# Fourier part of a small transformer: half-width token transform, then sum and difference of cosine and sine parts

## The chip, the cores and the metric

The kernel runs on one core of one Trainium2 chip. The metric is the device time of one execution in microseconds. The kernel before takes 1688.06 us, the median of three runs (1687.9 to 1688.19).

## The reference, cut to what matters

The program is four transformer blocks on one input sequence of 256 tokens and width 1024, in fp32. The first two blocks (layers 0 and 1) carry a context sequence of 256 tokens beside it; their mixer has three branches, whose outputs are joined and projected:

```python
fx = fourier_mix(col(ux, OFF_FOURIER, FOURIER_W), w_four[l])
ax, ac = attention_group(ux, uc, ...)
rx, rc = hgrn_group(ux, uc, ...)
x = x + g_a * (jnp.concatenate([fx, ax, rx], axis=-1) @ w_out[l])
```

The change touches the first branch only. It is a two-dimensional Fourier transform of a real input, over the 256 tokens and over the 64 features of each of four groups, of which the real part is kept, and then a product with a weight of 256 x 256:

```python
z = u.astype(jnp.float32).reshape(b, n, FOURIER_GROUPS, FOURIER_GD)
z = jnp.fft.fftn(z, axes=(1, 3), norm="ortho").real
return z.reshape(b, n, FOURIER_W).astype(u.dtype) @ w
```

In layer 0 it is computed for the context and for the input sequence, in layer 1 for the input sequence alone: three calls in all. The two later blocks have no Fourier part.

## The kernel before, in words

Matmul operands of the large products are split into a high and a low part (`split`, L170 on ScalarE and L171 on VectorE) and multiplied in three matmuls (`mm3`, L177 to L179). The Fourier part uses plain fp32 matmuls instead. Each fp32 matmul appears in the trace as two passes, each with a weight load of its own.

`mix1` builds layers 0 and 1. Its steps come in the order of the string `STEPS`: the recurrent branch (`z`, `h`), then `k`, `q`, `u`, `g` (projections; `u` fills the Fourier input `uf`), `m` (the output tile `mT`), `a` (attention) and `r` (`hgrn_read`, the read-out of the recurrent branch, whose transposes are L1312). The Fourier calls stand after all steps. Behind `mix1` comes the out projection, whose first two k tiles are the Fourier rows of `mT`; in layer 0 one more modulation job (`ada_late`, matmuls L321) stands between them in the program.

The order on each engine is not the program's. The tile framework takes, for each engine, the ready instruction that is first in the program, by its own estimate of durations; later work can so run ahead of earlier work that waits. The eight PSUM banks have fixed duties: `mm` 0 to 3 (products and attention scores), `tr` 4 and 5 (transposes), `ac` 6 (the attention's value products), `qk` 7. A bank is taken by `tr_bank()` or `qk_bank()` and is free again when its last reader is done.

The attention (`attention`, `softmax`, `pv`) works in sets of 512 score columns: scores L1512 into an `mm` bank, minimum L934 on VectorE, exponential L944 on ScalarE, reciprocal L955, scaling L959 (ScalarE) or L961 (VectorE), four transposes L897 into a `tr` bank, a copy to SBUF (L902 VectorE, L904 ScalarE). After four heads the passes of the value product L970 follow (8 for the context, 16 for the input sequence), and its split into `mT`. Layer 0 has 8 sets for the context and 16 for the input sequence, layer 1 has 16.

One Fourier call (`fourier`, L1063) has three products. The token transform (L1071) multiplies the 256 tokens of `uf` with the table `dft` of 256 cosine and 256 sine columns, in two halves of 128 features, each into bank 7 and from there by a copy into `a` (`foua`). The feature transform multiplies `a` with the block-diagonal tables `bd`: cosines (L1077) and, accumulating in the same bank, negated sines (L1078); a copy makes `z` (`fouz`). The weight product (L1084) follows in bank 7 again, and `split` writes the result to `mT`. `copy` (L164 or L166) alternates between ScalarE and VectorE from call to call.

Of the kernel before, what the change touches and what calls it, by code (L numbers as in the profile page):

```python
# [12 lines left out]
F32 = mybir.dt.float32  # L13
# [7 lines left out]
P = 128  # L21
# [26 lines left out]
def shape_constants():  # L48

    n = np.arange(SEQ)  # L50
    freqs = 10000.0 ** (-np.arange(0, 32, 2, dtype=np.float64) / 32)
    cos = np.zeros((SEQ, 64))
    sin = np.zeros((SEQ, 64))
    for off, pos in ((0, n // 64), (32, n % 64)):
        ang = pos[:, None] * freqs
        cos[:, off : off + 16] = cos[:, off + 16 : off + 32] = np.cos(ang)
        sin[:, off : off + 16] = -np.sin(ang)
        sin[:, off + 16 : off + 32] = np.sin(ang)
    ang = 2 * np.pi * ((n[:, None] * n[None]) % SEQ) / SEQ
    dft = np.concatenate([np.cos(ang), np.sin(ang)], 1)  # L60
    m = np.arange(64)
    ang = 2 * np.pi * ((m[:, None] * m[None]) % 64) / 64
    norm = 1.0 / math.sqrt(SEQ * 64)
    bd = np.zeros((P, 2, P))
    for g in range(2):
        s = slice(g * 64, g * 64 + 64)
        bd[s, 0, s] = np.cos(ang) * norm
        bd[s, 1, s] = -np.sin(ang) * norm
    t = np.arange(P) % 64
    mask = np.zeros((P, 7, 64), np.uint32)  # L70
    s_, t_ = t[:, None], m[None]
    for i, b in enumerate(LEVELS):
        mask[:, i] = (s_ // (2 * b) == t_ // (2 * b)) & (s_ // b != t_ // b)
    mask[:, 6] = s_ == t_
    dist = np.abs(n[:, None] - n[None])
    d_a = np.where(dist <= 128, dist, FAR)
    pos = np.arange(SEQ)
    tok = 2 * (pos % 128) + pos // 128
    dist = np.abs(tok[:, None] - tok[None])
    d_b1 = np.where(dist <= 64, dist, FAR)  # L80
    d4 = np.where(tok[:P, None] % 4 == tok[None, :P] % 4, dist[:P, :P], FAR)
    d16 = np.where(tok[:P, None] % 16 == tok[None, :P] % 16, dist[:P, :P], FAR)
    d_b23 = np.concatenate([d4, d16], 1)
    f = lambda a: np.ascontiguousarray(a, np.float32)
    return {
        "k_rope": f(np.stack([cos, sin], 1)),
        "k_dft": f(dft),
        "k_bd": f(bd),
        "k_mask": np.ascontiguousarray(mask),
        "k_dist": f(np.concatenate([d_a, d_b1], 1)),  # L90
        "k_dist2": f(d_b23),
    }


class Net:
# [967 lines left out]
    def fourier(self, pool, uf, tiles, mT, col0):  # L1063

        nc = self.nc
        mm = nc.tensor.matmul
        a = self.t(pool, [P, 2, 512], F32, "foua", bufs=1)
        for ft in range(2):
            ps = self.qk_bank()
            for i, tt in enumerate(tiles):  # L1070
                mm(ps, uf[:, tt, ft * P : ft * P + P], self.dft[:, i], start=i == 0, stop=i == 1)  # L1071
            self.copy(a[:, ft], ps)
        z = self.t(pool, [P, 2, 256], F32, "fouz", bufs=1)
        ps = self.qk_bank()
        for ft in range(2):
            o = ps[:, ft * 256 : ft * 256 + 256]
            mm(o, self.bd[:, 0], a[:, ft, :256], start=True, stop=False)  # L1077
            mm(o, self.bd[:, 1], a[:, ft, 256:], start=False, stop=True)  # L1078
        self.copy(z, ps.rearrange("p (f t) -> p f t", f=2))
        ps = self.qk_bank()  # L1080
        for ct in range(2):
            o = ps[:, ct * 256 : ct * 256 + 256]
            for k in range(2):
                mm(o, self.wf[:, k, ct * P : ct * P + P], z[:, k], start=k == 0, stop=k == 1)  # L1084
        cs = slice(col0, col0 + 256)
        self.split(mT[0][:, 0:2, cs], mT[1][:, 0:2, cs], ps.rearrange("p (f t) -> p f t", f=2))
# [268 lines left out]
    def mix1(self, hp, pool, l, hT, start=None, late=None):  # L1355
        nc, A = self.nc, self.A
# [23 lines left out]
        ps = []  # L1380
# [68 lines left out]
        v = self.t(pool, [P, 4, 128], F32, "v", bufs=1)  # L1449
# [78 lines left out]
        uf = gs_["uf"]  # L1528
        hes.close()
        with self.tc.tile_pool(name=f"four{l}", bufs=2) as ap:  # L1530
            self.dft = self.load(ap, "dft", [P, 2, 512], A["k_dft"].rearrange(
                "(t p) n -> p t n", p=P))
            self.bd = self.load(ap, "bd", [P, 2, P], A["k_bd"])
            self.wf = self.load(ap, "wf", [P, 2, 256], A["w_four"][l].rearrange(
                "(k p) n -> p k n", p=P))
            for seq in seqs:
                self.fourier(ap, uf, (2 * seq - t0, 2 * seq - t0 + 1), mT, seq * 256)
            if late is not None:
                for job in late(ap, (4,), 6):
                    for _ in job:  # L1540
                        pass
# [373 lines left out]
```

## Time and profile before

| | |
|---|---|
| time, median of three runs | 1688.06 us |
| the profiled execution | 1694.94 us |
| its span | 1693.1 us |
| PE busy | 1624.1 us (96%) |
| PE weight loads busy | 1342.8 us (79%) |
| VectorE busy | 1222.1 us (72%) |
| ScalarE busy | 855.8 us (51%) |
| mean DMA rate | 183 GB/s |

The page and the rows come from one profiled execution, which took a little longer than the timed runs. PE is the matmul engine, PEld its weight loads, DVE is VectorE, ACT is ScalarE, SPq the queue that issues DMAs. Matmuls are pipelined and their ends are modelled, so records of PE overlap, and its busy time is not the time at its peak.

### The profile page before, as it was taken

What the parts mean: (1) busy time and instruction counts of PE and PEld (TensorE: products, weight loads), DVE (VectorE), ACT (ScalarE), POOL (GpSimd) and SP (SyncE); (2) the same over time, 40 slices, a digit from 0 to 9 for tenths busy, and PEclk for the clock granted to TensorE, in tenths of its full rate; (3) what the DMA queues carried; (4) which work ended last, traced back from release to release, by engine and by line L of the source; (5) the groups of instructions that cost most, each with busy time, mean ns of one, the idle gap of its engine ahead of it and who ended that gap; (6) DMA issues with size and microseconds to landing.
All of it is one profiled execution on the core that took longest, in us unless ns stands there. A gap on an engine that the chain in (4) does not pass through costs nothing.

```text
span 1693.1 us, 27315 instructions
## 1 busy us (share of the span) xinstructions
PE 1624.1 (96%) x10343; PEld 1342.8 (79%) x10343; DVE 1222.1 (72%) x2042; ACT 855.8 (51%) x1697; POOL 45.0 (3%) x53
## 2 busy tenths in 40 slices
PE   7999899999999999899999999999999999889998
PEld 5777667877778877787678899777989988769896
DVE  4558866887978977878768887887776566575555
ACT  4446664533343334555755455686544456564443
POOL 0001100000000000101000000000000000000000
PEclk9999999999999999999999999999999999999999
DMA  9551425664678786522268897533876543255653
GB/s 325 185 175 32 154 76 175 188 193 144 225 233 302 265 267 201 161 85 79 82 198 291 311 312 238 163 124 123 277 249 184 184 133 93 77 175 168 204 176 112
DMA packets 169482, 310.48 MB, mean 183 GB/s; under 512 B 12163, under 2 KB 72819, under 8 KB 169350
## 3 DMA queue, kind: packets, MB, share of 16 engines
q1 hardware_dynamic: 168966, 308.17, 56.4%
q8 instruction: 81, 1.33, 0.3%
q10 hardware_dynamic: 384, 0.56, 0.1%
q14 instruction: 51, 0.42, 0.1%
HBM read 307.64 MB, written 1.05 MB: 182 GB/s over the span
## 4 chain that ended last, share of the span: by engine, by line
PE 69%; DMA 10%; DVE 10%; ACT 6%; issue 3%; POOL 1%; SPq 1%; ACTq 0%; POOLq 0%; DVEq 0%
PE bank L179 18%; PE bank L178 18%; PE bank L177 18%; DVE wlo L171 3%; ACT whi L170 3%; PE bank L970 2%; DMA raw<-w_up 2%; PE bank L897 2%; DMA raw<-ffn_w_in 2%; DMA raw<-w_gate 2%; DMA raw<-w_down 1%; ACT colj L387 1%; PE bank L1512 1%; PE bank L321 1%; DMA raw<-w_in 1%
## 5 line engine op out<-in xcount | busy, mean ns | idle before, releaser
L170 ACT CAST whi<-raw 128x1024 fp32r<-128x1024 f32 (+2 forms) x420 | 401.1, 959 | 524.0 <-PE bank L179 198.7
L171 DVE TENSOR_TENSOR wlo<-raw,whi 128x1024 fp32r<-128x1024 f32 (+2 forms) x420 | 464.4, 1110 | 257.0 <-ACT whi L170 247.3
L177 PE MATMUL bank<-hh,whi 128*128 128x256 f32 (+1 forms) x1240 | 386.3, 312 | 0.0
L178 PE MATMUL bank<-hl,whi 128*128 128x256 f32 (+1 forms) x1240 | 385.9, 311 | 0.0
L179 PE MATMUL bank<-hh,wlo 128*128 128x256 f32 (+1 forms) x1240 | 385.2, 311 | 0.2 <-DVE wlo L171 0.2
L177 PE MATMUL bank<-whi,hh 128*128 128x512 f32 (+2 forms) x720 | 265.6, 373 | 10.4 <-ACT hh L170 5.8
L178 PE MATMUL bank<-wlo,hh 128*128 128x512 f32 (+2 forms) x720 | 264.3, 368 | 2.1 <-DVE wlo L171 2.1
L179 PE MATMUL bank<-whi,hl 128*128 128x512 f32 (+2 forms) x720 | 262.5, 368 | 0.2 <-DVE hl L171 0.2
L178 PEld LDWEIGHTS bank<-hl,whi 128*128 128x128 f32 x1240 | 234.6, 189 | 14.8
L177 PEld LDWEIGHTS bank<-hh,whi 128*128 128x128 f32 x1240 | 234.5, 189 | 14.8
L179 PEld LDWEIGHTS bank<-hh,wlo 128*128 128x128 f32 x1240 | 234.1, 189 | 15.2 <-DVE wlo L171 0.4
L358 DVE SCALAR_TENSOR_TENSOR acc<-adaw,cs,acc 128x1024 f32<-128x1024 f32 x154 | 196.0, 1280 | 14.5 <-DMA adaw<-ada_w 6.8
L178 PE MATMUL bank<-wlo,acth 128*128 128x512 f32 x440 | 173.5, 394 | 0.5 <-DVE wlo L171 0.5
L177 PE MATMUL bank<-whi,acth 128*128 128x512 f32 x440 | 173.4, 395 | 0.0
L179 PE MATMUL bank<-whi,actl 128*128 128x512 f32 x440 | 173.3, 394 | 0.0
L177 PEld LDWEIGHTS bank<-whi,hh 128*128 128x128 f32 x720 | 136.7, 191 | 38.1 <-ACT hh L170 8.5
L179 PEld LDWEIGHTS bank<-whi,hl 128*128 128x128 f32 x720 | 137.4, 191 | 23.8 <-DVE hl L171 3.6
L178 PEld LDWEIGHTS bank<-wlo,hh 128*128 128x128 f32 x720 | 137.7, 191 | 21.8 <-DVE wlo L171 3.4
L178 PEld LDWEIGHTS bank<-wlo,acth 128*128 128x128 f32 x440 | 82.7, 188 | 19.2 <-DVE wlo L171 0.9
L179 PEld LDWEIGHTS bank<-whi,actl 128*128 128x128 f32 x440 | 82.9, 188 | 18.5
L177 PEld LDWEIGHTS bank<-whi,acth 128*128 128x128 f32 x440 | 82.8, 188 | 18.2
L756 DVE TENSOR_TENSOR rtmp<-bank,gate 128x512 f32<-128x512 f32 x68 | 46.5, 686 | 30.0 <-PE bank L179 30.0
(297 smaller groups left out, 1837.1 us busy)
## 6 DMA issues: line engine op xcount, KB each, us to landing
adaw<-ada_w SPq DMA_DIRECT2D x96, 512.0 KB
adaw<-w_ada SPq DMA_DIRECT2D x80, 512.0 KB
raw<-ffn_w_in SPq DMA_DIRECT2D x64, 512.0 KB
raw<-w_down SPq DMA_DIRECT2D x46, 512.0 KB
raw<-ffn_w_out SPq DMA_DIRECT2D x40, 512.0 KB
raw<-w_gate SPq DMA_DIRECT2D x32, 512.0 KB
raw<-w_up SPq DMA_DIRECT2D x32, 512.0 KB
raw<-w_in SPq DMA_DIRECT2D x56, 256.0 KB
```

The source lines that it names most:

```text
L170: a = self.nc.scalar.copy(hi, src)
L171: b = self.nc.vector.tensor_sub(lo, src, hi.bitcast(F32))
L177: mm(out, lh, rh, start=start, stop=False)
L178: mm(out, lh, rl, start=False, stop=False)
L179: mm(out, ll, rh, start=False, stop=stop)
L321: nc.tensor.matmul(ps[h][32 * g : 32 * g + 32], self.cs32[:, k0 + g], raws[g][:, h * 512 : h * 512 + 512], start=k0 == 0, stop=k0 > 0,)
L358: nc.vector.scalar_tensor_tensor(acc, raw, s, acc, op0=ALU.mult, op1=ALU.add)
L387: nc.scalar.activation(junk, ps[:, i * P : i * P + P], AF.Copy, accum_out=cols[:, k : k + 1])
L756: nc.vector.tensor_mul(tmp[:, :nw], ps[:, :nw], gate[:, n0 : n0 + nw])
L897: self.nc.tensor.transpose(ps[:, i * P : i * P + P], ps_in[:, i * P : i * P + P], self.ident)
L970: self.nc.tensor.matmul(o[e * 64 : e * 64 + 64], v, pt[:, e::2, i], start=i == 0, stop=i == len(vs) - 1)
L1512: nc.tensor.matmul(dst, q, ksT[:, i, kv, :nk], start=i == 0, stop=i == 1)
```

## The change

The table `dft` keeps 129 cosine columns (0 to 128) and 127 sine columns (1 to 127). The token transform therefore writes 256 columns for each half of the features, and both halves go to one bank and out of it in one copy. The feature transform writes the product of the cosine columns and that of the sine columns side by side, without accumulating, into a bank of the kind `tr` in place of `qk`. The sine part is copied to SBUF (`odd`) by ScalarE. VectorE copies columns 0 and 128, adds the two parts for columns 1 to 127 and subtracts them, read in reverse order, for columns 129 to 255. The weight product and the split are as before.

```diff
-    dft = np.concatenate([np.cos(ang), np.sin(ang)], 1)
+
+    dft = np.concatenate([np.cos(ang)[:, :129], np.sin(ang)[:, 1:128]], 1)
...
-        a = self.t(pool, [P, 2, 512], F32, "foua", bufs=1)
-        for ft in range(2):
-            ps = self.qk_bank()
-            for i, tt in enumerate(tiles):
-                mm(ps, uf[:, tt, ft * P : ft * P + P], self.dft[:, i], start=i == 0, stop=i == 1)
-            self.copy(a[:, ft], ps)
-        z = self.t(pool, [P, 2, 256], F32, "fouz", bufs=1)
+        a = self.t(pool, [P, 2, 256], F32, "foua", bufs=1)
         ps = self.qk_bank()
         for ft in range(2):
             o = ps[:, ft * 256 : ft * 256 + 256]
-            mm(o, self.bd[:, 0], a[:, ft, :256], start=True, stop=False)
-            mm(o, self.bd[:, 1], a[:, ft, 256:], start=False, stop=True)
-        self.copy(z, ps.rearrange("p (f t) -> p f t", f=2))
+            for i, tt in enumerate(tiles):
+                mm(o, uf[:, tt, ft * P : ft * P + P], self.dft[:, i], start=i == 0, stop=i == 1)
+        self.copy(a, ps.rearrange("p (f t) -> p f t", f=2))
+
+        z = self.t(pool, [P, 2, 256], F32, "fouz", bufs=1)
+        ps = self.tr_bank()
+        v = ps.rearrange("p (f t) -> p f t", f=2)
+        for ft in range(2):
+            mm(v[:, ft, :129], self.bd[:, 0], a[:, ft, :129], start=True, stop=True)
+            mm(v[:, ft, 129:], self.bd[:, 1], a[:, ft, 129:], start=True, stop=True)
+        odd = self.t(pool, [P, 2, 127], F32, "fouo", bufs=1)
+        nc.scalar.copy(odd, v[:, :, 129:])
+        nc.vector.tensor_copy(z[:, :, 0:129:128], v[:, :, 0:129:128])
+        nc.vector.tensor_add(z[:, :, 1:128], v[:, :, 1:128], odd)
+        nc.vector.tensor_sub(
+            z[:, :, 129:256], v[:, :, 1:128][:, :, ::-1], odd[:, :, ::-1]
+        )
         ps = self.qk_bank()
...
-            self.dft = self.load(ap, "dft", [P, 2, 512], A["k_dft"].rearrange(
+            self.dft = self.load(ap, "dft", [P, 2, 256], A["k_dft"].rearrange(
                 "(t p) n -> p t n", p=P))
```

## Rows read from the trace of the kernel before

**Rows 1.** The page, busy time of each engine, its share of the span and instructions.
```profile
PE 1624.1 (96%) x10343; PEld 1342.8 (79%) x10343; DVE 1222.1 (72%) x2042; ACT 855.8 (51%) x1697; POOL 45.0 (3%) x53
```

**Rows 2.** The page, the chain that ended last, share of the span by engine.
```profile
PE 69%; DMA 10%; DVE 10%; ACT 6%; issue 3%; POOL 1%; SPq 1%; ACTq 0%; POOLq 0%; DVEq 0%
```

**Rows 3.** Instructions on the Fourier tiles: duration ns min/median/max, first and last start us.
```profile
L1071 PE MATMUL bank<-dft,uf x24: 590/592/697, 195.7 to 830.0; 128*128 128x512 f32 x24
L242 SPq DMA_DIRECT2D dft<-k_dft x2: 367/394/422, 175.8 to 802.0; - x2
...
L1084 PE MATMUL bank<-fouz,wf x24: 378/379/382, 213.0 to 846.1; 128*128 128x256 f32 x24
...
L164 ACT COPY foua<-bank x3: 575/586/588, 198.4 to 823.2; 128x512 f32<-128x512 f32 x3
L166 DVE COPY foua<-bank x3: 674/682/692, 203.2 to 830.9; 128x512 f32<-128x512 f32 x3
...
L164 ACT COPY uf<-bank x3: 361/363/367, 191.0 to 812.9; 128x256 f32<-128x256 f32 x3
```

**Rows 4.** Windows: PE, PEld, DVE, ACT, POOL busy, PEclk, DMA share, GB/s.
```profile
195.60:245.30 49.70, 49.48 (x285) 31.43 (x285) 39.60 (x96) 39.77 (x105) 3.27 (x2) 1.00 0.06 21
...
816.10:848.30 32.20, 32.13 (x181) 20.23 (x181) 24.38 (x54) 22.59 (x51) 0.00 (x0) 1.00 0.10 33
```

**Rows 5.** The chain of waits in order of time: start us, us, what.
```profile
225.31 0.86 PE bank L1071 x2
...
245.78 0.44 PE bank L1312 x4
...
246.45 1.73 PE bank L1084 x8
248.17 4.17 PE bank L321 x24
...
846.45 1.89 PE bank L970 x14
```

**Rows 6.** Timeline, the read-out in layer 0: start us, us, engine, instruction.
```profile
202.27 0.67 DVE L1308 TENSOR_TENSOR hxh<-hxh,gs 128x512 f32<-128x512 f32 x1
...
242.43 0.60 PE L1312 MATMUL bank<-ident,hxh 128*128 128x128 f32 x4
```

**Rows 7.** Timeline, bank 7 between the two Fourier calls of layer 0.
```profile
194.00 0.41 DVE L166 COPY uf<-bank 128x256 f32<-128x256 f32 x1
...
222.15 0.68 DVE L171 TENSOR_TENSOR hl<-bank,hh 128x512 fp32r<-128x512 f32 x1
...
225.15 1.02 PE L1071 MATMUL bank<-dft,uf 128*128 128x512 f32 x2
```

**Rows 8.** Groups by form, 195 to 248 us, VectorE reading a bank.
```profile
L171 DVE TENSOR_TENSOR hl<-bank,hh 128x256 fp32r<-128x256 f32 x8 | 3.3, 418 | 0.7 <-ACT hh L170 0.6
```

**Rows 9.** Timeline, layer 0, Fourier passes beside attention copies.
```profile
235.89 0.58 ACT L904 COPY pt<-bank 128x512 f32<-128x512 f32 x1
...
236.17 1.02 PE L1071 MATMUL bank<-dft,uf 128*128 128x512 f32 x2
...
239.10 0.69 DVE L902 COPY pt<-bank 128x512 f32<-128x512 f32 x1 [1.71 <-PE bank L970]
...
239.49 0.60 PE L1077 MATMUL bank<-foua,bd 128*128 128x256 f32 x2
```

**Rows 10.** Timeline, layer 1, start of the out projection (idle before and its releaser).
```profile
849.73 0.74 PE L177 MATMUL bank<-whi,hh 128*128 128x512 f32 x2 [1.41 <-ACT whi L170]
...
850.99 0.50 PE L178 MATMUL bank<-wlo,hh 128*128 128x512 f32 x1 [0.53 <-DVE wlo L171]
```

**Rows 11.** Windows in and behind layer 1's out projection, columns as in rows 4.
```profile
852.00:854.00 2.00, 2.00 (x6) 1.57 (x5) 1.21 (x2) 0.00 (x0) 0.00 (x0) 0.50 0.89 261
854.00:856.00 2.00, 2.00 (x7) 1.53 (x7) 0.25 (x1) 1.04 (x1) 0.00 (x0) 0.64 0.93 280
...
870.00:880.00 10.00, 8.16 (x41) 6.19 (x40) 7.37 (x15) 6.98 (x17) 1.11 (x2) 1.00 0.36 105
```

## The prediction

> **What bounds the kernel now.** I read the page first: PE is busy for 96% of the span [rows 1] and holds 69% of the chain that ended last [rows 2]. So a shorter matmul can shorten the kernel, but only where no other wait stands right behind it. Next I asked for the instructions on the Fourier tiles: the token transform (L1071), the feature transform (L1077, L1078) and the weight product (L1084) run from 195.7 us in layer 0 (context and input sequence) and up to 846.1 us in layer 1 (input only) [rows 3]. Both places lie inside the attention. There PE reads 49.48 of 49.70 us busy in layer 0 and 32.13 of 32.20 us in layer 1, ScalarE and VectorE 70 to 80% [rows 4]. The chain of waits in these stretches runs through PE in small pieces, Fourier matmuls among them [rows 5].
>
> The timeline then says why they can stand there. The read-out of the recurrent part (L1307, L1308, then transposes L1312) is ahead of the Fourier part in the program. The input of its transposes is written at 202.27 us, and they run at 242.43 [rows 6]; layer 1 has the same picture. PE's order does not hold them, for L1071, later in the program, runs all the while. They need a "tr" bank (4 or 5), and those go round in program order among the attention's transposes, 24 sets in layer 0 and 16 in layer 1. The Fourier part uses bank 7 ("qk") alone, which the attention does not touch here, so it fills the pauses. Bank 7 itself is handed on in program order: the context's result leaves it at 222.15 + 0.68 = 222.83 us, and the first token transform of the input sequence follows at 225.15, though its operand uf was written at 194.00 [rows 7].
>
> **The change, part by part.** *Matmuls.* An fp32 matmul shows as two passes: 24 records for the 12 calls of L1071 [rows 3]. In the chain a pass of 512 columns takes 0.86/2 = 0.43 us, one of 256 columns 1.73/8 = 0.216 us, one of 128 columns 0.44/4 = 0.11 us [rows 5]. For one sequence the token transform falls from 8 x 0.43 = 3.44 to 8 x 0.216 = 1.73 us, the feature transform from 1.73 to 8 x 0.11 = 0.88 us. No row has 129 or 127 columns or an odd start; a pass lies between 0.11 and 0.216 us, and I take 0.11, the row of nearly the same width. Saved: 1.71 + 0.85 = 2.56 us a sequence, 7.7 us of PE work in all.
>
> *Copies and loads.* The copies of a fall from two of 512 elements (0.59 us on ScalarE, 0.68 on VectorE) to one, and that of z goes [rows 3]. In come a ScalarE copy of 254 elements, nearest row 0.363 us for 256 out of a bank [rows 3]; a VectorE copy of four columns, at most the 0.418 us of 256 [rows 8] and beside the ScalarE copy; and an add and a subtract of 254, nearest the same 0.418. The reversed read has no row; I bound it by 0.418 and twice that, and take 0.418. The load of dft falls from 512 to 256 KB; it is issued at 802.0 us in layer 1 [rows 3], some 17 us ahead of its use, so this gains nothing.
>
> *The new place of the feature transform.* It now takes a "tr" bank, and by [rows 6] gets one only after all attention transposes and the read-out. The weight product waits for it and holds bank 7 from the copy of a on; by [rows 7] the input sequence's chain in layer 0 then waits for the context's. So the feature transforms and weight products move from inside the attention to behind it, and in layer 0 the input sequence's token transform as well. Next comes the out projection, whose first k tiles are the Fourier rows; nothing of it can start sooner.
>
> *What the attention gets back.* Layer 0: its attention holds 16 passes of 0.43, 16 of 0.216 and 8 of 0.216 us (the context's weight product), 12.1 us; 1.7 stay, 10.4 go. The return lies between 0 (only pauses were filled) and 10.4. I followed two of them. A pair of L1071 at 236.17 (to 237.19) holds back the value product, whose last operand was copied at 235.89 + 0.58 = 236.47: 0.65 us. The pair ahead of it costs an estimated 0.24 more, so about 0.9 of 1.72 comes back, 52%. The pair of L1077 at 239.49 costs at most 0.1, for the next transposes wait for the copy that ends at 239.10 + 0.69 = 239.79 anyway [rows 9]. I take 52% for the 7.0 us ahead of 231 us, 0.9 + 0.1 for the rest, and 0.4 for the copies: 5.0 us. Layer 1: 5.2 us go; the last group of heads returns nothing (it waits on its own copies), the one before 0.4, the token transform half of 1.71, the copies 0.2: 1.5 us.
>
> By the matmul rows alone PE is full and all 10.4 + 5.2 us would come back. The Trainium skill (Perfetto Trace Analysis, "Identifying the Most-Contended Engine") warns that matmul busy time is a poor measure, since matmuls are pipelined, and asks for the share of weight loads: 31.43 of 49.70 us, 63% [rows 4]. The trace agrees: a pass that takes 0.216 us of the chain is recorded as 0.379 [rows 3, 5]. By the first reading the sum would be -6.9 us, by the second it is the one below.
>
> *What is added behind it.* Layer 1: after the last value product (846.45 + 1.89 = 848.34 [rows 5]) come the feature transform 0.88 + 0.16 for the end of its last pass, the ScalarE copy 0.41, add and subtract 0.82, weight product 1.73 + 0.2, the split's first half 0.65: 4.85 us to the out projection's first matmul. Today that starts at 849.73, stops after two matmuls for wlo and goes on at 850.99 [rows 10], as if it had started at 850.5, 2.2 us behind. The weight splits that hold it today then lie under the chain. Added: 2.6 us. Layer 0: PE gets 0.88 twice, 1.73 and 1.73 = 5.2 us behind the attention. Of the context's chain (4.85 and the read-out's 0.44 = 5.3 us) PE fills 0.44 + 0.88 + 1.73 and eight passes of L321 at 4.17/24 each [rows 5], 1.4 us; 0.9 us is empty. The second chain lies under the context's out projection. Added: 6.1 us.
>
> *Sum.* Layer 0: -5.0 + 6.1 = +1.1; layer 1: -1.5 + 2.6 = +1.1; together +2.2 us. The profiled execution took 1694.94 us (span 1693.1 and 1.84 around it), so 1697.1 for its like; it lies 6.9 us above the median of the timed runs, 1688.06, and the difference carries over: 1690.3 us.
>
> **The rivals.** *Faster: the attention gives most of it back.* For it: the full PE rows [rows 4], and that each pass gone frees those behind it. Against it: the pair at 239.49. At 80%: layer 0 -8.3 + 6.1, layer 1 -4.2 + 2.6, together -3.8 us: 1684.3; at 100%, -6.9: 1681.2. On the same side lies that "tr" banks are not handed out in program order, and the chain stays inside the attention: 45 to 100% of 7.7 us, 1680.4 to 1684.6. Against that stands the 40 us wait of L1312 [rows 6].
>
> *Clearly slower: a serial tail and the clock.* One mechanism: PE stands idle behind the attention while ScalarE and VectorE make z. If the attention returns only 20% (2.1 and 1.0 us) the tails leave +4.0 and +1.6. On top, the granted clock: behind today's pause for whi and wlo it is 0.50 (1.2 GHz) from 852 to 854 us and 0.64 to 856 [rows 10, 11]; that is 3.4 us at half speed, 1.7 lost. A second such stretch in layer 0 makes +7.3 in all, 1695.4. It decides from a return of about a third down. Against it: at 870 to 880 us PE is idle for 1.84 us and the clock stays at 1.00 [rows 11]. The skill (TensorE: Matmul & The Clock Gate, "HAM oscillation — how this bites in real kernels") has it that bursts with waits between them fall back to the low clock time after time; by that rule the new pauses are paid twice.
>
> **How the numbers follow.** My own case 0.50 (its own range 1686 to 1693.5), the faster rival 0.22, the slower one 0.28. About 0.2% (3.4 us) is what a measurement of this kernel can tell from no change. My case lies 2.2 us above the old median, so 0.07 of it goes to slower and 0.02 to faster, and 0.03 of the faster rival stays within: faster 0.21, within 0.2% 0.44, slower 0.35. The range, 1683.5 to 1695.5, takes in the main figures of both rivals and leaves out the ends, about 0.2.
>
> **What would show it.** Right: L1312 still near the end of the attention and the new L1077/L1078 behind it; in layer 1 the first L177 of the out projection about 5 us behind the last value product; layer 0's attention 4 to 6 us shorter. Wrong: a feature transform in the middle of the attention (bank order); an attention shorter by 8 us or more (PE really full); a pass of 129 columns well over 0.11 us; a second stretch at the low clock.

## The result, and the profile after

The changed kernel takes 1701.39 us (median of 4 runs, 1699.42 to 1705.57) against 1687.98 beside it: ratio 1.0073, 95% interval 1.0052 to 1.0094. Timed once more with other runs of the kernel before (`e8_after_again`) it is 1.0070, 1.0057 to 1.0083, or 11.8 us more (9.6 to 14.0). I had forecast 2.2 us more and a range that ended at 1695.5: the prediction was wrong, in the size and in the class it held likeliest.

The page of the changed kernel, engines and then the chain by engine, answers to [rows 1] and [rows 2] and hardly differs: PE is busy 4.5 us less.

```profile
PE 1619.6 (95%) x10343; PEld 1339.6 (79%) x10343; DVE 1222.7 (72%) x2048; ACT 854.7 (50%) x1697; POOL 45.4 (3%) x53
...
PE 69%; DVE 10%; DMA 9%; ACT 7%; issue 4%; POOL 1%; SPq 0%; ACTq 0%; POOLq 0%; DVEq 0%
```

Lines up to the Fourier part have moved down by one; the token transform is L1073 now, the feature transform L1080 and L1081, the weight product L1093. Instructions on the Fourier tiles of the changed kernel, columns as in [rows 3]:

```profile
L1073 PE MATMUL bank<-dft,uf x24: 377/379/483, 198.1 to 836.2; 128*128 128x256 f32 x24
...
L1080 PE MATMUL bank<-foua,bd x12: 275/276/378, 247.5 to 858.4; 128*128 128x129 f32 x12
...
L1081 PE MATMUL bank<-foua,bd x12: 272/273/274, 247.8 to 858.6; 128*128 128x127 f32 x12
...
L1093 PE MATMUL bank<-fouz,wf x24: 379/379/796, 250.9 to 864.3; 128*128 128x256 f32 x24
L1084 DVE COPY fouz<-bank x3: 154/157/168, 249.9 to 860.3; 128x4 f32<-128x4 f32 x3
L1085 DVE TENSOR_TENSOR fouz<-bank,fouo x3: 412/413/413, 250.0 to 860.4; 128x254 f32<-128x254 f32 x3
L1086 DVE TENSOR_TENSOR fouz<-bank,fouo x3: 412/414/414, 250.3 to 860.7; 128x254 f32<-128x254 f32 x3
```

Apart from layer 1's weight product, of which more below, no instruction is clearly dearer than I took it: the subtract that reads in reverse takes 414 ns, the add 413. And the first starts show the move: no feature transform before 247.5 us, no weight product before 250.9.

Windows of the changed kernel, columns as in [rows 4]: the two attentions, each from its first exponential to the end of its last value product, then the stretch behind layer 0's.

```profile
198.43:247.56 49.13, 41.88 (x253) 25.85 (x251) 37.42 (x91) 37.66 (x101) 4.12 (x2) 1.00 0.05 18
822.00:857.76 35.76, 31.01 (x185) 19.62 (x183) 25.08 (x58) 24.96 (x56) 1.64 (x1) 1.00 0.17 56
...
247.56:266.00 18.44, 17.77 (x94) 12.06 (x94) 5.96 (x12) 3.85 (x8) 0.00 (x0) 1.00 0.43 149
```

The same stretches in the trace of before (to the same two instructions):

```profile
196.09:245.34 49.25, 49.10 (x285) 31.17 (x283) 39.15 (x95) 39.29 (x104) 3.27 (x2) 1.00 0.06 18
812.22:848.32 36.10, 34.71 (x200) 22.31 (x199) 26.51 (x60) 25.97 (x58) 1.64 (x1) 1.00 0.16 56
```

This is the result in four lines: 7.2 us of PE's busy time left layer 0's attention (49.10 to 41.88), and the attention got 0.12 us shorter; in layer 1 3.7 us left it for 0.34. Where the time went is in the groups by line of PE in layer 0's attention of the changed kernel (the last column is PE's idle time before them and what ended it). Nearly all of it is new: before, PE was idle for 0.15 us in this stretch.

```profile
L898 PE MATMUL bank<-ident,prob 128*128 128x128 f32 x96 | 15.2, 282 | 1.9 <-ACT prob L960 1.6 <-DVE pt L903 0.3
L971 PE MATMUL bank<-pt,v 128*64 128x256 f32 x96 | 14.7, 390 | 2.3 <-ACT pt L905 1.2 <-DVE pt L903 1.1
L1521 PE MATMUL bank<-ksT,qsT 128*128 128x512 f32 x32 | 12.3, 454 | 3.1 <-ACT prob L945 3.1
```

What was taken out came back as waits for exponentials (3.1 us), copies (2.6) and divisions (1.6). ScalarE and VectorE are not alone in setting the pace: in the chain of waits over this attention, PE's own attention matmuls hold 58% (L971, L898, L1521), ScalarE 31%, VectorE 4%. First line: the changed kernel, 198.43 to 247.56 us; second: before, 196.09 to 245.34.

```profile
by line: PE bank L971 28.9%; ACT prob L945 21.0%; PE bank L898 18.0%; PE bank L1521 11.3%; issue 5.5%; ACT pt L905 4.9%; ACT prob L960 4.8%; DVE pt L903 2.5%; DVE stat L935 1.4%; ACT foua L165 1.0%; DVE stat L956 0.5%; ACTq L945 0.1%; ACTq 
...
by line: PE bank L970 28.3%; PE bank L897 23.8%; PE bank L1512 20.3%; PE bank L1071 14.5%; PE bank L1084 2.6%; PE bank L1077 2.6%; ACT prob L944 2.6%; PE bank L1078 1.8%; issue 1.6%; ACT pt L904 1.0%; PE bank L177 0.9%; PE bank L1312 0.9%; 
```

Before, the Fourier passes (L1071, L1077, L1078, L1084) held 21% of this chain, some 10 us, and still nothing was won by taking most of them out: where PE finds work to fill a wait, the chain runs through that work.

The chain of waits of the changed kernel, where [rows 5] stand: start us, us, what. The exponential, the copies of the probabilities and PE take turns up to the end of the attention; then the read-out, the transforms and both weight products follow in a row, the second token transform among them.

```profile
242.06 0.79 ACT prob L945 x2
...
243.03 0.65 DVE pt L903
...
244.99 0.59 ACT pt L905
...
245.62 1.94 PE bank L971 x14
247.56 0.42 PE bank L1080 x2
247.99 0.22 PE bank L1081 x2
248.21 0.44 PE bank L1321 x4
248.64 0.23 PE bank L1080 x2
...
250.93 1.94 PE bank L1093 x8
252.89 0.59 ACT hh L171
...
254.72 1.73 PE bank L1073 x8
...
260.02 1.79 PE bank L1093 x8
```

The same chain behind layer 1's attention, where the out projection (L178, before: [rows 10]) now starts at 865.34, 7.6 us behind the last value product:

```profile
858.06 1.06 ACT whi L171
...
859.14 0.31 DVE wlo L172
859.46 0.83 issue
860.29 0.11 DVE fouz L1084
...
860.69 0.42 DVE fouz L1086
...
861.15 3.52 PE bank L1093 x8
864.70 0.59 ACT hh L171
...
865.34 0.50 PE bank L178
```

The timeline of the same place shows a weight split on VectorE (`wlo`, 1.22 us) between the sine part and the four columns, and a weight product of 3.51 us in place of layer 0's 1.94. PE had stood idle for 2.31 us before it, and it runs for the most part at a granted clock of 0.50, 1.2 GHz (windows in the part on the prediction).

```profile
859.01 0.38 ACT L1083 COPY fouo<-bank 128x254 f32<-128x254 f32 x1
859.14 1.22 DVE L172 TENSOR_TENSOR wlo<-raw,whi 128x1024 fp32r<-128x1024 f32 x1 [0.52 <-ACT whi L171]
...
861.15 3.51 PE L1093 MATMUL bank<-fouz,wf 128*128 128x256 f32 x8 [2.31 <-DVE fouz L1086]
```

**Where the loss is.** I set the start of the same PE instruction in both traces side by side: the first score matmul of each attention, one in layer 0's feed-forward (313.59 us before) and one in layer 1's (892.30). From the first score to the instruction in the feed-forward is called a layer's stretch below.

| kernel | first score, layer 0 | feed-forward | first score, layer 1 | feed-forward | longer by, layer 0 | layer 1 |
|---|---|---|---|---|---|---|
| before | 192.57 | 313.59 | 806.63 | 892.30 | | |
| after | 194.91 | 322.40 | 816.39 | 905.28 | +6.48 | +3.23 |
| after again | 193.08 | 320.32 | 813.95 | 902.94 | +6.22 | +3.32 |

The two stretches hold 9.5 to 9.7 us. The profiled pair lies 13.0 us apart at the last of these instructions and only 4.5 at the end (spans 1697.6 and 1693.1). Some 5 of these 8.5 us are stretches at the lower clock, which fall differently in every execution (last section): behind 900 us the trace of before has four of 1.7 us, the changed kernel's one, not counting the last 10 us. The rest was not followed; the timed runs are the measure of the whole.

### The profile page after: what moved, and what is told of

It reads as the page before. It is cut to its first block, busy times and chain, and to the rows that moved or that the text cites. A ratio compares the mean times of both kernels' runs of the same rounds, so it can differ in the third digit from the quotient of the medians.

```text
span 1697.6 us, 27328 instructions
## 1 busy us (share of the span) xinstructions
PE 1619.6 (95%) x10343; PEld 1339.6 (79%) x10343; DVE 1222.7 (72%) x2048; ACT 854.7 (50%) x1697; POOL 45.4 (3%) x53
## 4 chain that ended last, share of the span: by engine, by line
PE 69%; DVE 10%; DMA 9%; ACT 7%; issue 4%; POOL 1%; SPq 0%; ACTq 0%; POOLq 0%; DVEq 0%
PE bank L180 19%; PE bank L178 19%; PE bank L179 19%; DVE wlo L172 3%; ACT whi L171 3%; PE bank L971 2%; DMA raw<-w_up 2%; DMA adaw<-w_ada 2%; PE bank L898 1%; DMA raw<-ffn_w_in 1%; DVE acc L359 1%; ACT prob L945 1%; ACT colj L388 1%; PE bank L322 1%; DMA raw<-w_gate 1%
## 5 line engine op out<-in xcount | busy, mean ns | idle before, releaser
L178 PE MATMUL bank<-hh,whi 128*128 128x256 f32 (+1 forms) x1240 | 385.7, 311 | 0.0
L178 PE MATMUL bank<-whi,hh 128*128 128x512 f32 (+2 forms) x720 | 265.6, 373 | 11.0 <-ACT hh L171 7.1
L178 PEld LDWEIGHTS bank<-hh,whi 128*128 128x128 f32 x1240 | 233.7, 188 | 14.8 <-DVE rtmp L757 0.2
L178 PE MATMUL bank<-whi,acth 128*128 128x512 f32 x440 | 173.7, 395 | 0.0
L178 PEld LDWEIGHTS bank<-whi,hh 128*128 128x128 f32 x720 | 136.8, 191 | 38.3 <-ACT hh L171 10.4
L178 PEld LDWEIGHTS bank<-whi,acth 128*128 128x128 f32 x440 | 82.8, 188 | 18.6
```

The costliest lines, as they stand in the source:

```text
L178: mm(out, lh, rh, start=start, stop=False)
```

## The experiments

Theory 1: the bank `tr`, given in program order, moved the transforms behind the attention, and the attention, set by ScalarE and VectorE, gave nothing back for it. Theory 2: the new small operations cost the time. Theory 3: mine, half comes back.

**One word back in the changed kernel (`e1_z_in_qk`).**

```
-        ps = self.tr_bank()
+        ps = self.qk_bank()
```

> The changed kernel with one word changed: the sums of the feature transform take a bank of the group that the token transform takes ("qk"), not of the group that the attention's transposes rotate through ("tr"); every instruction stays. Theory 1 (the bank): with the bank given in program order the transforms and weight products went from beside the attention to behind it, and that is the whole loss; so here the feature transforms stand beside the attention again, the out projection of layer 0 starts within 1 us of the last read-out transposes, and the time is 1685 to 1690 us (ratio 0.998 to 1.001). Theory 2 (the new small operations, the odd widths, the reversed reads): they are all still there, so the loss stays, 1694 to 1701 us (ratio 1.004 or more). Theory 3 (my forecast: half of the PE work taken out beside the attention comes back): 1684 us, with a layer 0 attention of about 45 us.

Measured: ratio 0.9994 (0.9980 to 1.0008). All new operations and widths are still in it, so theory 2 is out: the whole loss hangs on the bank. What is left of the change is worth 1.0 us, between 3.4 us less and 1.4 us more, which can't be told from nothing. The attention is no shorter here either; PE's time went from 49.10 to 46.71 us in it:

```profile
199.14:248.46 49.32, 46.71 (x292) 31.50 (x291) 39.32 (x98) 38.25 (x104) 3.27 (x2) 1.00 0.04 13
```

**The bank alone, in the kernel before (`e2_before_z_in_tr`)**: `tr_bank()` for its feature transform.

> The kernel before with one word changed: its feature transform takes a bank of the group of the attention's transposes; widths, passes and copies are those of before. Theory 1 (the bank): its PE work behind layer 0's attention is larger than the changed kernel's (two feature transforms, the second token transform and two weight products: 1.73 x 2 + 1.73 + 3.44 = 8.6 us against about 5.2), so it loses at least as much: 1701 to 1706 us (ratio 1.008 or more). Theory 2 (the new small operations): nothing of them is here, 1688 us (ratio 0.999 to 1.001).

Measured: 1.0076 (1.0059 to 1.0093); in the trace layer 0's stretch is 9.66 us longer, layer 1's 0.88. One word, and no Fourier arithmetic changed, makes the loss of the whole change. Layer 0 loses more than in the changed kernel, as its larger matmuls ask; that layer 1 loses less I had not expected (1.7 us of it is a low clock stretch that this execution doesn't have and the one of before has). These two runs don't tell whether the transform waits for its bank while the kernel runs, or was put behind the attention in PE's order when the kernel was built; either way the bank decides.

**No transforms at all (`e3_no_transforms`).** The token and the feature transform are left out, z is a copy of uf.

> The kernel before without its token transform and feature transform: the weight product reads a copy of the Fourier input instead, so the Fourier output is another one than the reference's. It takes 5.2 us of PE work per pair out of the time beside the attention (two pairs in layer 0, one in layer 1). Theory 1 (the attention goes by its own chain through ScalarE and VectorE, so that PE work taken out comes back as idle PE): the stretch of the layer 0 attention stays 49 to 50 us long, layer 1's about 32 us, and the span falls by less than 2 us. Theory 3 (half of it comes back): layer 0's stretch 44 to 45 us, layer 1's 29 to 30 us, the span 7 to 8 us shorter.

Measured: one run, 1685.84 us, within the runs of before beside it (1683.97 to 1692.12). The attention, without 5.2 us of PE work per pair (the two transforms of one call), is not shorter but 2.1 us longer, 51.39 us (layer 1: 36.72, at a mean clock of 0.95):

```profile
196.77:248.16 51.39, 47.75 (x284) 30.97 (x283) 37.88 (x91) 37.54 (x102) 3.27 (x2) 1.00 0.05 16
```

Yet layer 0's whole stretch is 3.89 us shorter, which theory 1 as I put it (under 2 us for the span) did not have. The instructions of the modulation job, which stand behind the Fourier part in program order, say where from: before, all start from 248.1 us on; here 12 of the 32 stand in the attention, and with them 16 passes of the out projection (counted in the timeline).

```profile
L321 PE MATMUL bank<-adaw,cs x32: 592/593/617, 225.4 to 260.0; 128*32 128x512 f32 x32
```

So work taken out of a stretch that is filled up pays only by what can move in from behind it. PE stayed filled here (47.75 us), so this run alone doesn't settle whether PE's work sets the length. The changed kernel, `e2` and `e4` are plainer: next to nothing moved in, PE is busy for 42 to 43 us, and the attention keeps its 49.1. Nor is all filling free: ScalarE and VectorE had less to do than before, and yet the attention took 2.1 us longer. Why was not followed.

**`tr` in layer 0 alone (`e4_tr_layer0_only`)**: `self.tr_bank() if uf.shape[1] == 4 else self.qk_bank()` in the changed kernel.

> The changed kernel with the bank of the changed kernel ("tr") in layer 0 alone and the token transform's group ("qk") in layer 1; nothing else differs. Theory 1 (the bank): the loss of layer 0 alone, by the two traces about 6 us, and none in layer 1: 1693 to 1696 us, and together with the kernel that has it nowhere and the changed kernel this splits the loss about two to one between the layers. Theory 2 (the new small operations): the same time as the changed kernel, 1699 to 1702 us.

Measured: 1.0039 (1.0024 to 1.0054), 1694.78 us; layer 0's stretch +6.13 us in the trace, layer 1's -2.25 (the low clock stretch of before is missing here too). The loss is split as the traces say, some 6.6 us (4.1 to 9.1) of 11.8 in layer 0.

**A bank that comes free earlier (`e5_z_in_mm`)**: `self.mm_bank()` in the changed kernel.

> The changed kernel with the feature transform's sums in a bank of the group that the attention's score tiles take ("mm", four banks); nothing else differs. In the trace of the changed kernel the last score tile of layer 0 is at 236.6 us, the last value product at 247.6. Theory 1 (the bank is given in program order, and what comes behind the attention is paid in full): the transforms are now released some 11 us before the attention's end, where TensorE has pauses of about 1 us in 6, so most of the loss goes: 1688 to 1692 us (ratio 1.000 to 1.002), between the kernel with the bank "qk" and the changed one. Rival (the place of the bank is not what decides, but that the transforms share a group with the attention at all): near the changed kernel, 1697 us or more.

Measured: 1.0037 (1.0021 to 1.0054), clearly more than I expected. Layer 1, with one call, loses nothing (-0.20 us); layer 0 still loses 4.97 of the changed kernel's 6.2 to 6.5. PE's timeline in layer 0 shows why: the first feature transform starts 11 us before the end of the attention, the last passes of its weight product only at 247.84, and only then comes the second token transform.

```profile
236.91 0.49 PE L1080 MATMUL bank<-foua,bd 128*128 128x129 f32 x2 [0.42 <-ACT prob L945]
...
242.27 1.03 PE L1093 MATMUL bank<-fouz,wf 128*128 128x256 f32 x4
...
247.84 0.60 PE L1093 MATMUL bank<-fouz,wf 128*128 128x256 f32 x2
...
251.54 1.89 PE L1073 MATMUL bank<-dft,uf 128*128 128x256 f32 x8
```

The second call waits for bank 7 ([rows 7] show the same hand-over before), so in layer 0 a bank that is early for the first call is still late for the second. In the kernel of `e1` the first feature transform does not wait for a shared bank, and the second weight product ends 1.9 us behind the attention (250.39 us) instead of 14 (261.81). So an earlier start of the first transform gave back little by itself; what layer 0 still loses goes, by this timeline, to the second call, which follows the first on bank 7. It is not sharing a bank with the attention as such, for layer 1 shares and loses nothing. The number of calls in a row was not varied by itself.

**Is it ScalarE and VectorE (`e6_after_no_scale`, `e7_before_no_scale`)?** The division of the probabilities by their row sums is left out in the mixers with the Fourier part, in both kernels. Its rows in layer 0 of before, which also correct the counts in the expectation (32 in layer 0, 16 in layer 1):

```profile
L959 ACT ACTIVATE prob<-prob,stat x16: 495/616/726, 197.5 to 237.7; 128x256 f32<-128x256 f32 x8, 128x512 f32<-128x512 f32 x8
L961 DVE TENSOR_SCALAR prob<-prob,stat x16: 335/410/486, 198.1 to 241.2; 128x256 f32<-128x256 f32 x8, 128x512 f32<-128x512 f32 x8
```

> The changed kernel without the division of the probabilities by their row sums in the mixers with the Fourier part (64 small multiplications on ScalarE and VectorE in layer 0, 32 in layer 1), so the output is another than the reference's. Theory 1 (the attention's length is set by its chain through ScalarE and VectorE, and TensorE waits for it): from the first exponential to the last value product layer 0 takes 43 us or less instead of 49.1, layer 1 31 to 33 instead of 35.8, and TensorE's pauses inside shrink. Theory 3 (the attention's length is TensorE's): 48 to 49 us as now.

> The kernel before without the same multiplications. Here TensorE was busy in 49.48 of 49.70 us, with work of the Fourier part in the pauses. Theory 1: the attention gets shorter here too although TensorE looked full, 43 to 45 us in layer 0, because part of the Fourier work is fill that falls behind the attention instead. Theory 3 (a full TensorE is the bound): 48 to 49 us, unchanged.

Measured: 43.71 and 43.45 us in layer 0 (the first a little more than the 43 expected), 31.32 and 31.72 in layer 1. Windows of the attentions, first of the changed kernel without the division, then of the one before:

```profile
199.85:243.56 43.71, 40.08 (x252) 25.50 (x250) 29.57 (x72) 28.50 (x84) 3.58 (x2) 1.00 0.06 21
820.14:851.46 31.32, 28.96 (x184) 19.36 (x183) 21.43 (x49) 19.47 (x47) 1.64 (x1) 1.00 0.20 64
```

```profile
198.20:241.65 43.45, 42.58 (x260) 26.76 (x259) 30.15 (x73) 29.00 (x85) 3.58 (x2) 1.00 0.06 19
817.51:849.23 31.72, 30.33 (x184) 19.30 (x183) 22.16 (x50) 19.46 (x47) 1.64 (x1) 1.00 0.20 64
```

Layer 0's attentions shrink by much the same, 5.4 and 5.8 us, and the one of before is 98% full of PE in 43.45 us after 99.7% in 49.25. A PE that is full at the shorter length too did not set the longer one: the divisions stand in the chain, and what does not fit goes behind. Whether PE's own attention matmuls would bound a still shorter attention is not shown (40.08 of 43.71 us are busy in the changed kernel without the division). What goes behind costs again: the kernel before without the division has its last weight product from 255.4 us on, 14 us behind the attention, and its layer 0 stretch is 2.87 us longer than with it. The whole took 1698.44 us in one run (with the division 1691.76, up to 1697.06), the changed kernel without it 1691.43; single runs are too few to price that.

**Latency or load (`e9` to `e12`)?** All four are the kernel of `e1`, with the division put on other engines: a quarter on GpSimd, half on GpSimd, a quarter instead of half on ScalarE, all on VectorE.

```
+            if self.pool_share and heads[i] % 4 in self.pool_share:
+                nc.gpsimd.tensor_scalar_mul(pt[:, s], pt[:, s], r[:, i : i + 1])
```

> The changed kernel with the feature transform's bank in "qk", and in the mixers with the Fourier part every fourth head's division of the probabilities by the row sums (half of VectorE's) put on GpSimd, which stood nearly idle there (about 4 us of 49). Theory 1 (the attention's length is set by ScalarE and VectorE, and TensorE's work in it is fill): leaving all 64 divisions out took 5.4 us off the layer 0 attention; a quarter of them elsewhere gives back up to a quarter of that, 1 to 1.5 us per layer, if GpSimd's own operation is not later than VectorE's 0.41 us (256 columns) or 0.5 us (512): ratio to the kernel before 0.997 to 1.000. If GpSimd's operation is much longer (over 2 us), it is the late link of the chain, and the attention gets longer: ratio 1.000 to 1.005.

> The same with half of the divisions (one of ScalarE's and one of VectorE's of each four heads) on GpSimd. Theory 1 with a short GpSimd operation: 2 to 2.7 us off each attention, ratio 0.996 to 0.999. With a long one: twice the loss of the kernel with a quarter.

> The changed kernel with the feature transform's bank in "qk", and in the mixers with the Fourier part only every fourth head's division on ScalarE instead of every second one; VectorE takes the others. In the trace of before one division takes 0.495 to 0.726 us on ScalarE and 0.335 to 0.486 us on VectorE. Theory 1, as the GpSimd runs sharpened it (the attention's length is the latency of its chain, so that one link's duration counts, not an engine's load): 8 links of layer 0 get some 0.2 us shorter, 0 to 1.6 us off its attention, half of it off layer 1's; ratio 0.997 to 1.000. If VectorE's load counts instead (it is 5.0 to 6.0 of 6 us busy in the first half), the attention gets longer by up to the 8 x 0.41 = 3.3 us that move to it; ratio 1.000 to 1.003.

> The same with all divisions on VectorE. Theory 1 by latency: 0 to 3 us off the layer 0 attention, ratio 0.996 to 1.000. If VectorE's load counts: up to 16 x 0.41 = 6.6 us more, ratio 1.001 to 1.006.

| kernel | layer 0's attention, us | VectorE, ScalarE busy in it | ratio (95%) |
|---|---|---|---|
| e1, half ScalarE, half VectorE | 49.32 | 39.32, 38.25 | 0.9994 (0.9980 to 1.0008) |
| e9, a quarter on GpSimd | 53.01 | 36.50, 38.76 | 1.0045 (1.0029 to 1.0061) |
| e10, half on GpSimd | 54.55 | 36.35, 33.89 | 1.0045 (1.0030 to 1.0060) |
| e11, a quarter on ScalarE | 51.60 | 42.62, 34.81 | 0.9996 (0.9980 to 1.0013) |
| e12, none on ScalarE | 51.81 | 41.78, 29.45 | 1.0020 (1.0005 to 1.0036) |

The GpSimd case is the dear one of the two expected, though half on GpSimd does not lose twice as much as a quarter: with less work on VectorE (in `e10` on ScalarE too) the attention got longer, because one link did. Instructions on the probabilities in layer 0 with a quarter on GpSimd, and idle time that its end released (us, times):

```profile
L962 POOL TENSOR_SCALAR prob<-prob,stat x8: 923/1562/1719, 202.9 to 247.5; 128x256 f32<-128x256 f32 x4, 128x512 f32<-128x512 f32 x4
...
  POOL prob L962: 8.2, 8
```

So the latency of a link counts. But latency alone failed at `e11`: links got shorter, VectorE 3.3 us busier, and the attention 2.3 us longer; and load alone does not explain `e12`, which moved twice as many divisions and is only 0.2 us longer still. Besides, the passes that fill PE's waits changed with the divisions (in `e11` all 16 of the weight products stand in the attention, in `e1` 11), and that alone may lengthen it, as `e3` suggests. Which link sets the length at which place stays open. That the kernel of `e11` is no slower for its longer attention fits the filling: less of the weight products is left behind it. No version beats the kernel before.

**The changed kernel again (`e8_after_again`).**

> The changed kernel once more, beside the same runs of the kernel before. The two traces place 6.2 us of loss in layer 0 and 3.5 in layer 1, 9.7 in all (ratio 1.0057); the first timing gave 1.0073 with 1.0052 to 1.0094. Theory 1 as it stands: 1.0045 to 1.0075. If it is 1.008 or more, some 4 us of the loss are elsewhere and not found yet.

Measured: 1.0070 (1.0057 to 1.0083). The traces' 9.5 to 9.7 us in the two stretches, with the 0.6 to 0.9 between them 10.1 to 10.7, lie inside the 9.6 to 14.0 us of the timing; a further 1 or 2 us elsewhere can't be told from nothing.

## Why the prediction was wrong

- *What bounds the kernel.* Wrong at the root for this stretch. PE full in [rows 4] was read as a bound that is loosened in part. PE's waits had been filled with Fourier passes, and the attention runs at the pace of its own chain, in which PE's attention matmuls, ScalarE and VectorE take turns. The sentence of the Trainium skill that I weighed (Perfetto Trace Analysis, "Identifying the Most-Contended Engine") warned of reading matmul busy time that way. I followed it to the share of weight loads, and its 63% led me no further than "not all comes back"; it fell to 53% (25.85 of 49.13 us) in an attention of the same length, so it did not tell what bounds this stretch.
- *What the attention gets back* is the step that failed. 5.0 us in layer 0 and 1.5 in layer 1 were forecast; 0.12 and 0.34 came. I had followed one pair of passes that held back a value product by 0.65 us [rows 9] and taken 52% from it for all. What one such place gives back, PE then waits for at the next, for an exponential, a copy or a division (7.3 us before the attention's matmuls in the changed kernel, 0.1 in the kernel before). Six kernels with 41.8 to 49.1 us of PE work in the same 49.1 to 49.5 us (before, after, `e1`, `e2`, `e4`, `e5`) show that such delays did not add up to a longer attention.
- *The new place of the feature transform* was right in all: behind the read-out's bank, both weight products after it, the second token transform behind the attention too (254.56). `e1` and `e2` show that this is the whole cause.
- *Prices of passes and copies* were right: in the chain two passes of 129 columns take 0.23 us and two of 127 take 0.22, apart from the first two of all (0.42).
- *What is added behind it.* Layer 0: 6.1 us forecast, 6.3 to 6.6 measured (the stretch's 6.2 to 6.5 and the 0.12 returned). Layer 1: 2.6 forecast, 3.6 to 3.7 measured (3.2 to 3.3 and 0.34). I had left out that VectorE stands in a weight split (wlo, from 859.14) when the sine part is ready at 859.39; the four columns were copied at 860.29, 0.9 us late. The out projection starts 7.6 us behind the last value product where I had summed 4.85; besides the 0.9, 1.6 us of that is the weight product at the lower clock, which drops out of the difference, for before the out projection lost 1.7 in the same way [rows 11].
- *The sum* with the returns measured would have been -0.12 + 6.1 - 0.34 + 2.6 = +8.2, 1696.3 us, just above my range; the rest is layer 1's tail and what the trace doesn't place.
- *Rivals.* The slower one was nearest, and its first half, a return of a fifth or less, was what happened. Its second half was not: layer 0 got no low clock (1.00, which is 2.4 GHz, from 247.56 to 266 us), and in layer 1 the low stretch only moved, from the out projection [rows 11] into the weight product ahead of it, as the windows of the changed kernel below show. Nor does such a pause always bring one: in `e4` PE stands idle at the start of layer 1's out projection for 1.41 and 0.52 us, as before [rows 10], and the clock is 1.00 in the whole stretch (814.11 to 897.52). By the rule that I took from the Trainium skill (TensorE: Matmul & The Clock Gate, "HAM oscillation — how this bites in real kernels") the pauses would have been paid twice; here they were paid once. That page tells of a loop that waits for a DMA at every step, for longer than the 2.31 us here; no run here has such waits.

```profile
860.00:862.00 2.00, 0.85 (x2) 0.76 (x3) 2.00 (x5) 1.27 (x2) 0.00 (x0) 0.71 0.10 10
862.00:864.00 2.00, 2.00 (x6) 1.56 (x6) 1.37 (x2) 0.00 (x0) 0.00 (x0) 0.50 0.70 264
```

- *The chances.* Half for my own case rested on an interpolation between 0 and 10.4 us with two places followed; the lower bound had the better mechanism behind it.

## What to carry to other kernels

An engine that is busy to the last tenth, and holds most of the chain, may be full of work that only fills its waits: before a saving there is priced, ask whether the stretch would be any shorter without all of it, and whether anything behind can move in. A buffer that is handed out in program order is a place in time: a transform that takes one from a group that other work rotates through starts where that work ends. And calls that follow one another on one bank hand such a delay on: in `e5` layer 0, with two, still lost 4.97 us, layer 1, with one, nothing.

## What was not expected of the hardware

The reversed read of a bank cost nothing: 414 ns for 254 columns, 413 for the add in plain order. GpSimd took 923 to 1719 ns for the multiplication that takes VectorE 335 to 486 (256 and 512 columns; of 512 alone 1562 to 1563 in this attention, and spans on GpSimd are rough). And the stretches at the lower clock (0.50, 1.2 GHz) cost 1.7 us each or twice that (above: 2 us at 0.71 and 2 us at 0.50, with 0.1 after them) and lie at other places in each execution; in windows of 4 us over the span without its last 10 us I count some 13.5 us lost to them in the trace of before, 10.1 in the changed kernel's, 15.2 in that of `e5_z_in_mm` and 6.8 in that of `e4_tr_layer0_only`. The difference of two spans of single executions can so be off by up to 8 us (15.2 less 6.8); the length of one stretch between two instructions is the better measure.
